# A two-layer diffusion-transformer step: modulation matmuls between the input's transposes, and head norms with an operand in PSUM

## The chip, the cores and the metric

The kernel runs on one core of one Trainium2 chip. The metric is the device time of one execution in microseconds (us). A core has five engines that run their own instruction queues and meet through semaphores: TensorE (PE: matmuls and transposes, into PSUM), VectorE (DVE), ScalarE (ACT: activation functions, casts), GpSimd (POOL) and SyncE (SP, which here issues the DMAs). A measurement of this kernel is the median of several runs.

## The reference

The reference is one step of a hybrid diffusion backbone: two layers, 1024 sample tokens and 128 prompt tokens of width 1024, all in float32. What bears on the change:

```python
def _rms(x, g):
    y = xf * lax.rsqrt(jnp.mean(xf * xf, axis=-1, keepdims=True) + EPS)
    return (y * g).astype(x.dtype)

def _modulation(cvec, w, b):
    m = (jax.nn.silu(cvec) @ w + b)[:, None, :]
    return jnp.split(m, 6, axis=-1)

def _layer(x, mod, lw, ctx):
    sh1, sc1, g1, sh2, sc2, g2 = mod
    h = _rms(x, n1) * (1 + sc1) + sh1
    u_conv, qa, ka, va, qn, kn, vn = jnp.split(h @ w_in, idx, axis=-1)
    a_out = _conv_module(u_conv, dw_w, dw_b, ln_g, ln_b)
    qa = _rms(qa.reshape(B, L, GQA_HEADS, HEAD_DIM), aqg)
    ka = _rms(ka.reshape(B, L, GQA_KV_HEADS, HEAD_DIM), akg)
    qn = _rms(qn.reshape(B, L, NA_HEADS, HEAD_DIM), nqg)
    kn = _rms(kn.reshape(B, L, NA_HEADS, HEAD_DIM), nkg)
    ...
    x = x + g1 * (jnp.concatenate([a_out, b_out, c_out], axis=-1) @ w_out)
    h = _rms(x, n2) * (1 + sc2) + sh2
    x = x + g2 * (jnp.square(jax.nn.relu(h @ w1)) @ w2)
```

So the modulation (a vector-matrix product with a 1024 x 6144 weight, for the sample's and the prompt's conditioning) must be known before the first projection, and every head of q and k is normalised by the root mean square of its 64 channels. The depthwise convolution has 31 taps over 256 channels.

## The kernel before

**Layout.** The residual X lies transposed in SBUF: 8 tiles (one for each 128 channels, index k) with all 1152 tokens along the free dimension. Tokens form three segments: si 0 and si 1 with 512 sample tokens each, si 2 with the 128 prompt tokens. Matmuls run on operands split in a high part and a low part (`wh`, `wl`, `HA` tiles): ACT casts the high part, and another engine subtracts it to get the low part (`split`, L155 on). The tiles come from pools with a fixed number of slots (S, T, U, V in SBUF; eight PSUM banks under one tag, `P`). A new tile waits until the slot's last user is done.

**The order** of instructions on each engine is the order of the Python program: there is no scheduler. Generators are advanced by `next` where their piece of work is to stand, and every engine works through its own queue in that order.

**The prologue** (`prologue`, L343) does the following, in this order.

- It issues the loads: four tiles `xt` with the first half of the sample, four `xh` with the second half (in slots HF 8 to 11 of a set of 16 buffers), two `xtp` for the prompt, then the weight of the first third of the modulation (`ada_w`, 16 loads of 512 KB into the HF buffers). As `xh` and the last four of these 16 share buffers, the last loads wait until PE has transposed `xh`.
- `x_in` (L331) brings in a segment. For each of 8 k: PE transposes 4 blocks (1 for the prompt) into a PSUM tile `psx`, VectorE copies it to X (L338), and `Norm.add` squares X on ACT and adds the square to an accumulator. There are two accumulators `nacc` a segment, for even and odd k. The even one is added by POOL, the odd one by VectorE; the first square of each is written to it directly.
- `modulation(0, [0], True)` (L183) multiplies: 8 steps of 4 matmuls into `psmod` (2 rows each). Then VectorE copies `psmod` to `mt` (L229), PE transposes it to `psmt`, VectorE adds the bias (`mod`) and forms `A1`.
- `Norm.rstd` (L272) adds the two accumulators, sums over the channels with a matmul against ones (`psn`), takes Ln and Exp on ACT (`rsq_start`), and improves the root in three VectorE operations (`rsq_end`).
- `pr.prep` splits weight tiles for the first projection (`wr` to `wh`, `wl`); the first is split with POOL. Then `norm1` writes the normalised input (`nx`, `HA`), and the first projection (`psf`) starts.

The order is: all of `x_in` for the three segments, then four modulation steps, the norms' matmuls, four more modulation steps; meanwhile ACT and VectorE take the roots.

**The projection** (`project`, L689) of a layer has 35 groups: seven column blocks (`ORDER`: A0 to A5, VN) x five token groups (`GROUPS`: four of 256 tokens, one of 128). A group is a chain of matmuls into `pst` (L541 to L543). For 30 of the groups `post` calls `head_stats` and `head_norm` (L415, L425): ACT squares `pst`, VectorE sums over each head (`ss`, L420), ACT takes Ln and Exp into `y`, VectorE improves the root in three small operations on 128x8 or 128x4 elements (`nt`, `y`) and multiplies (`xn`, L99). POOL applies gains and the rotary tables (`o`), and the result goes to DRAM (`ddA`), from where the attention reads it back (`kd`).

Between the two halves of `post` stand the taps of the convolution (`conv_tap`): on VectorE a scalar_tensor_tensor over 128x1167 (`cacc`), and for 22 taps of the second channel half an ACT product (`cp`) with an addition on POOL (L570). Every second group advances `fill`, the modulation of the remaining two thirds, by one step (`aw` loads, `psmod`, `mt`, `psmt`).

`rsq_end`, which the head norms and the token norms share, is:

```python
    def rsq_end(q, y, t, m):
        stt(t, y, -0.5 / m, y, ALU.mult, ALU.mult)
        stt(t, q, EPS * m, t, ALU.add, ALU.mult)
        stt(y, t, 1.5, y, ALU.add, ALU.mult)
```

Of the kernel before, what the change touches and what calls it, by code (L numbers as in the profile page):

```python
# [14 lines left out]
ACTF = mybir.ActivationFunctionType  # L15
ALU = mybir.AluOpType
# [9 lines left out]
DH = 64  # L26
EPS = 1e-6
# [18 lines left out]
def hybrid_step(ctx, tc, I, O, depth=DEPTH):  # L46
    nc = tc.nc
# [10 lines left out]
    def S(shape, dt=F32, n="s"):  # L58
        return pers.tile([128] + list(shape), dt, tag="S", bufs=N_S, name=nm(n))
# [7 lines left out]
    def V(shape, n="v"):  # L67
        return pers.tile([128] + list(shape), F32, tag="V", bufs=24, name=nm(n))
# [18 lines left out]
    def P(n="ps"):  # L87
        return psum.tile([128, 512], F32, tag="p", bufs=8, name=nm(n))
# [3 lines left out]
    def act(out, in_, func, scale=1.0, bias=0.0, **k):  # L92
        nc.scalar.activation(out=out, in_=in_, func=func, scale=scale, bias=bias, **k)  # L93
# [7 lines left out]
    def stt(out, a, s, b, op0, op1):  # L101
        nc.vector.scalar_tensor_tensor(out=out, in0=a, scalar=s, in1=b, op0=op0, op1=op1)  # L102
# [7 lines left out]
    eps = pers.tile([128, 1], F32, name="eps")  # L110
# [32 lines left out]
    def load(out, in_, eng=None):  # L143
        (eng or nc.sync).dma_start(out=out, in_=in_)
# [17 lines left out]
    def rsq_start(q, y, m):  # L162

        act(y, q, ACTF.Ln, scale=1.0 / m, bias=eps)
        act(y, y, ACTF.Exp, scale=-0.5)
# [6 lines that stand above are left out]
# [11 lines left out]
    def modulation(l, groups, first=False):  # L183

        todo = [(r, k) for r in groups for k in range(KT)]
        ready = []

        def fetch():
            if todo:
                r, k = todo.pop(0)  # L190
                if first:
                    if k % 2 == 0:
                        o = {0: 0, 2: 12, 4: 4, 6: 8}[k]
                        ready.extend([[HF[o + 2 * a + b][:, c:c + 512] for b in range(2) for c in (0, 512)] for a in range(2)])
                    o = {0: 0, 2: 12, 4: 4, 6: 8}[k - k % 2] + 2 * (k % 2)
                    for b in range(2):
                        c = r * 2048 + b * 1024
                        load(HF[o + b][:, 0:1024], I["ada_w"][l, k * 128:(k + 1) * 128, c:c + 1024])
                    return
                four = []  # L200
                for c in range(r * 2048, (r + 1) * 2048, 512):
                    aw = T([512], n="aw")
                    load(aw, I["ada_w"][l, k * 128:(k + 1) * 128, c:c + 512])
                    four.append(aw)
                ready.append(four)

        for _ in range(6 if first else 1):
            fetch()
        if first:
            ps = P("psmod")  # L210
            nc.vector.memset(ps, 0.0)
            yield
            fetch()
            fetch()
        yield
        for r in groups:
            if not first:
                ps = P("psmod")
                nc.vector.memset(ps, 0.0)
                yield  # L220
            for k in range(KT):
                aw = ready.pop(0)
                for j in range(4):
                    mm(ps[32 * j:32 * j + 2, :], silc[:, k, :], aw[j], start=(k == 0), stop=(k == KT - 1))
                if not first:
                    fetch()
                yield
            mt = T([512], n="mt")
            nc.vector.tensor_copy(mt, ps)  # L229
            yield  # L230
            pt = P("psmt")
            for b in range(4):
                nc.tensor.transpose(pt[:, b * 128:(b + 1) * 128], mt[:, b * 128:(b + 1) * 128], ident)
            ptv = pt.rearrange("p (b j x) -> p j b x", b=4, j=4, x=32)
            for s in range(2):
                tt(mod[l][:, s, r * 16:(r + 1) * 16].rearrange("p (j b) -> p j b", j=4), ptv[:, :, :, s],
                   ada_b(l)[:, r * 16:(r + 1) * 16].rearrange("p (j b) -> p j b", j=4), ALU.add)
            if r == 0:
                for s in range(2):
                    stt(A1[l][:, s, :], mod[l][:, s, 8:16], 1.0, n1g(l), ALU.add, ALU.mult)  # L240
            if r == 2:
                for s in range(2):
                    stt(A2[l][:, s, :], mod[l][:, s, 32:40], 1.0, n2g(l), ALU.add, ALU.mult)
            yield
# [75 lines left out]
    def run(g):  # L320
        for _ in g:
            pass
# [8 lines left out]
    def x_in(si, xt, nrm):  # L331

        n = SEGS[si][1]
        for k in range(KT):
            ps = P("psx")
            for i in range(n // 128):
                nc.tensor.transpose(ps[:, i * 128:(i + 1) * 128], xt(i, k), ident)
            nc.vector.tensor_copy(xs(k, si), like(si, ps[:, 0:n]))  # L338
            nrm.add(k)
            if k % 2:  # L340
                yield

    def prologue(pr):  # L343
        nc.scalar.preload_act_table_set("natural_log_exp_and_others")
        make_identity(nc, ident)
        nc.vector.memset(ones, 1.0)
        nc.vector.memset(eps, EPS)
        cc = U([KT, 2], n="cc")
        xt = [S([1024], n="xt") for _ in range(4)]
        for i in range(4):  # L350
            load(xt[i], I["x_sample"][i * 128:(i + 1) * 128, :])
        load(cc, I["cc"])
        load(vecs[0], I["vecs"][0])
        xh = [HF[8 + i][:, 0:1024] for i in range(4)]
        for i in range(4):
            load(xh[i], I["x_sample"][(i + 4) * 128:(i + 5) * 128, :])
        xp = [T([512], n="xtp") for _ in range(2)]
        for b in range(2):
            load(xp[b], I["x_prompt"][:, b * 512:(b + 1) * 512])
        m0 = modulation(0, [0], True)  # L360
        next(m0)
        sg = U([KT, 2], n="sg")
        sigmoid_of(sg, cc)
        tt(silc, cc, sg, ALU.mult)
        norms = [Norm(si) for si in range(3)]
        for k in range(KT):
            X[k] = S([2, HT], n="X")
        run(x_in(0, lambda i, k: xt[i][:, k * 128:(k + 1) * 128], norms[0]))
        del xt
        run(x_in(1, lambda i, k: xh[i][:, k * 128:(k + 1) * 128], norms[1]))  # L370
        next(m0)
        pr.fetch()
        pr.fetch()
        run(x_in(2, lambda i, k: xp[k // 4][:, k % 4 * 128:(k % 4 + 1) * 128], norms[2]))
        del xp
        for _ in range(4):
            next(m0)
        gs = [nrm.rstd() for nrm in norms]
        for _ in range(2):
            for g in gs:  # L380
                next(g)
        run(gs[0])
        for _ in range(2):
            next(m0)
        pr.prep(nc.gpsimd)
        for _ in range(2):
            pr.fetch()
        load(colmask, I["colmask"])
        for l in range(1, depth):
            load(vecs[l], I["vecs"][l])  # L390
        spill(0, 0)
        spill(0, 1)
        run(m0)
        first = norm1(pr.L, 0, norms[0], True)
        next(first)
        pr.prep()
        run(first)
        for g in gs[1:]:
            run(g)
        pr.prep()  # L400
        yield
        yield from together(norm1(pr.L, 2, norms[2], True), norm1(pr.L, 1, norms[1], True))
# [12 lines left out]
    def head_stats(x, nt):  # L415
        n = nt * (x.shape[2] // 64)
        sq = T([nt, x.shape[2]], n="sq")
        act(sq, x, ACTF.Square)
        ss = V([n], "ss")
        nc.vector.tensor_reduce(out=ss, in_=sq.rearrange("p t (h d) -> p (t h) d", d=64), op=ALU.add, axis=AX.X)  # L420
        y = V([n], "y")
        rsq_start(ss, y, DH)
        return x, nt, n, ss, y

    def head_norm(x, nt, n, ss, y):  # L425
        rsq_end(ss, y, V([n], "nt"), DH)
        w = x.shape[2]
        xn = T([nt, w], n="xn")
        tt(heads4(xn, nt), heads4(x, nt), y.rearrange("p (t h) -> p t h", t=nt).unsqueeze(3).to_broadcast([128, nt, w // 64, 64]), ALU.mult)
        return xn  # L430
# [1365 lines left out]
    def spill(l, t):  # L1796
        for k in range(KT):
            load(dx[l][:, k, t * HT:(t + 1) * HT], X[k][:, t, :])
# [12 lines left out]
    with tc.manual_schedule():  # L1811
        L = begin_layer(0)
        pr = Projection(L)
# [3 lines left out]
        for l in range(depth):  # L1817
# [22 lines left out]
            pr = Projection(N)  # L1840
# [142 lines left out]
```

## Time and profile before

| | us |
|---|---|
| median of 3 runs | 2981.17 |
| lowest, highest | 2978.42, 2985.02 |
| the profiled execution | 2982.7 |
| its span, first to last instruction | 2980.9 |
| prologue's last accumulator addition ends | 36.2 |
| first ACT write of the normalised input (`HA`) | 47.17 |
| first matmul of the first projection (`psf`) | 47.94 |
| projection's token groups, layer 0 | about 105 to 360 |
| projection's token groups, layer 1 | about 1600 to 1850 |

PE's mean granted clock over the span is 0.983 of full speed. The page's times are those of one execution; a span of the trace is 1.8 us shorter than what the execution was timed at.

In the rows of the profile, `mt<-psmod` reads: writes mt, reads psmod; then come partitions x elements and the type, and how many such instructions were merged in the row. A bracket at a row's end gives the idle time of the engine ahead of it and what ended it. In a group's row, three durations are the shortest, the median and the longest in ns.

### The profile page before, as it was taken

How to read it: one execution, taken by the hardware profiler on the slowest of the kernel's cores; microseconds unless marked ns; L12 is line 12 of the kernel's file. 1: busy time of each engine (PE TensorE's matmuls, PEld its weight loads, DVE VectorE, ACT ScalarE, POOL GpSimd, SP SyncE). 2: the span in 40 equal slices, each digit the busy share in tenths (PEclk: the TensorE clock that was granted, in tenths of full speed). 3: DMA queues.
4: the chain of work that ended last, by engine and by line, in shares of the span. 5: the costliest groups of instructions: out<-in, count | busy, mean ns of one | idle time of the engine just before them, and what ended most of it. 6: DMA issues, size and time to landing. Idle time of an engine off the chain costs nothing.

```text
span 2980.9 us, 52857 instructions
## 1 busy us (share of the span) xinstructions
PE 2844.0 (95%) x20328; PEld 2525.2 (85%) x20328; DVE 2096.1 (70%) x4009; ACT 1401.0 (47%) x2864; POOL 652.5 (22%) x607
## 2 busy tenths in 40 slices
PE   6998999999999999999889989999999999999999
PEld 3878745789999989999868886458999999999999
DVE  6588778764867756768675877788557677585676
ACT  4333356762744443433452353668537444433343
POOL 3576345420000000000224772463100000000000
PEclk8999999999999999999999999999999999999999
DMA  7276302424466678443333672024245666565334
GB/s 286 85 210 167 106 20 61 102 65 139 148 212 198 208 239 300 161 156 96 122 129 106 187 200 75 16 55 111 89 124 179 207 203 196 201 236 183 116 102 161
DMA packets 434876, 444.05 MB, mean 149 GB/s; under 512 B 120512, under 2 KB 308672, under 8 KB 434624
## 3 DMA queue, kind: packets, MB, share of 16 engines
q1 hardware_dynamic: 434624, 440.67, 47.4%
q8 instruction: 160, 2.62, 0.4%
q14 instruction: 92, 0.75, 0.1%
HBM read 307.41 MB, written 133.17 MB: 148 GB/s over the span
## 4 chain that ended last, share of the span: by engine, by line
PE 76%; DVE 13%; ACT 4%; issue 2%; DMA 2%; POOL 2%; SPq 1%; DVEq 0%; POOLq 0%; ACTq 0%
PE ps L1319 23%; PE psb L1319 8%; PE psc L1319 6%; PE pso L1319 5%; PE psa L1319 5%; PE psd L1319 3%; PE psacc L1118 3%; PE pspv L985 2%; DVE cacc L102 2%; PE pspt L969 2%; PE pst L541 2%; PE pst L542 2%; PE pst L543 2%; PE psst L1132 2%; PE psm L1044 2%
## 5 line engine op out<-in xcount | busy, mean ns | idle before, releaser
L1319 PE MATMUL ps<-ts,w2h 128*128 128x288 f32 x3072 | 534.4, 296 | 8.3 <-DVE ts L99 4.8
L1319 PEld LDWEIGHTS ps<-ts,w2h 128*128 128x128 f32 x3072 | 451.7, 189 | 9.3 <-DVE ts L99 5.3
L1319 PE MATMUL ps<-ts,w2l 128*128 128x288 f32 x1536 | 329.2, 295 | 0.1
L96 ACT CAST ts<-ti 128x576 fp32r<-128x576 f32 x256 | 172.1, 672 | 310.2 <-PE ps L1319 208.6
L541 PE MATMUL pst<-wh,HA 128*128 128x256 f32 x1040 | 297.9, 286 | 0.0
L542 PE MATMUL pst<-wl,HA 128*128 128x256 f32 x1040 | 294.3, 283 | 0.2 <-DVE wl L99 0.2
L543 PE MATMUL pst<-wh,HA 128*128 128x256 f32 x1040 | 293.7, 282 | 0.0
L93 ACT ACTIVATE ev<-ev 128x576 f32<-128x576 f32 x240 | 164.7, 686 | 265.1 <-DVE ev L99 261.3
L1319 PEld LDWEIGHTS ps<-ts,w2l 128*128 128x128 f32 x1536 | 247.6, 189 | 0.4 <-DVE w2l L99 0.3
L102 DVE SCALAR_TENSOR_TENSOR X<-ps,mod,X 128x288 f32<-128x288 f32 x336 | 112.2, 410 | 163.5 <-PE ps L1319 163.5
L99 DVE TENSOR_TENSOR ts<-ti,ts 128x576 fp32r<-128x576 f32 x256 | 195.5, 764 | 44.7 <-ACT ts L96 44.7
L541 PEld LDWEIGHTS pst<-wh,HA 128*128 128x128 f32 x1040 | 198.3, 191 | 19.2 <-issue 6.9
L542 PEld LDWEIGHTS pst<-wl,HA 128*128 128x128 f32 x1040 | 198.2, 191 | 0.5 <-DVE wl L99 0.4
L543 PEld LDWEIGHTS pst<-wh,HA 128*128 128x128 f32 x1040 | 198.2, 191 | 0.0
L99 POOL TENSOR_TENSOR nacc<-nacc,nsq 128x512 f32<-128x512 f32 (+1 forms) x12 | 15.8, 1320 | 822.2 <-PE ps L1319 796.3
L1772 POOL COPY yu<-X 128x128 f32<-128x128 f32 x8 | 3.9, 500 | 836.2 <-DVE X L102 824.3
L1319 PE MATMUL pso<-HA,woh 128*128 128x288 f32 x1024 | 177.8, 295 | 0.0
L1046 DVE TENSOR_REDUCE mx<-psm 128x1 f32<-128x384 f32 x288 | 142.3, 547 | 30.1 <-PE psm L1044 30.0
L93 ACT ACTIVATE pt<-psst 128x512 f32<-128x512 f32 x216 | 118.1, 597 | 89.6 <-PE psst L1133 88.7
L99 POOL TENSOR_TENSOR R<-R,pt 128x1024 f32<-128x1024 f32 x60 | 148.3, 2472 | 26.3 <-ACT pt L93 24.3
L1319 PEld LDWEIGHTS pso<-HA,woh 128*128 128x128 f32 x1024 | 149.7, 188 | 0.0
L102 DVE SCALAR_TENSOR_TENSOR cacc<-cin,vecs,cacc 128x1167 f32<-128x1167 f32 x78 | 136.8, 1754 | 11.3 <-POOL cacc L570 10.1
(279 smaller groups left out, 7222.6 us busy)
## 6 DMA issues: line engine op xcount, KB each, us to landing
ti<-hd SPq DMA_DIRECT2D x128, 576.0 KB, 4.0
hd<-ev SPq DMA_DIRECT2D x224, 288.0 KB, 4.2
w1r<-in_mlp_w SPq DMA_DIRECT2D x176, 256.0 KB, 4.0
aw<-in_ada_w SPq DMA_DIRECT2D x160, 256.0 KB, 4.0
HF<-in_mlp_w SPq DMA_DIRECT2D x128, 256.0 KB, 5.3
ddA<-o SPq DMA_DIRECT2D x144, 128.0 KB, 3.0
wr<-in_w_in SPq DMA_DIRECT2D x28, 512.0 KB, 4.1
sd<-ev SPq DMA_DIRECT2D x24, 576.0 KB, 2.8
```

The costliest lines, as they stand in the source:

```text
L93: nc.scalar.activation(out=out, in_=in_, func=func, scale=scale, bias=bias, **k)
L96: nc.scalar.copy(out, in_)
L99: (eng or nc.vector).tensor_tensor(out=out, in0=a, in1=b, op=op)
L102: nc.vector.scalar_tensor_tensor(out=out, in0=a, scalar=s, in1=b, op0=op0, op1=op1)
L541: mm(o, hi, wh, start=(k == 0), stop=False)
L542: mm(o, hi, wl, start=False, stop=False)
L543: mm(o, lo, wh, start=False, stop=(k == KT - 1))
L969: nc.tensor.transpose(ps[0:n, c], self.p[j][:, o:o + n], ident)
L985: mm(ps[64 * j:64 * j + 64, 0:128], v[j], self.at[j, i], start=(i == 0), stop=(i == nb - 1))
L1046: nc.vector.tensor_reduce(out=mx[j][:, qt, b:b + 1], in_=ps[:, 0:384], op=ALU.max, axis=AX.X)
L1118: mm(acc[64 * j:64 * j + 64, :], v, pt[:, j, :], start=(kt == 0), stop=(kt == 8))
L1319: mm(ps[h][:, 0:HH], x, y[:, h * HH:(h + 1) * HH], start=(start and z == 0), stop=(stop and z == 2), skip_group_check=True)
```

## The change

In the prologue, `xh` gets four tiles of its own, so that all modulation loads can be issued at once. The modulation's steps stand between pairs of k of the second and third `x_in`: four steps in the second segment, two in the third, and two later. The norms' additions both go to VectorE. The accumulators of the first segment are added before the third `x_in`; the other two follow after it, then all Ln and Exp. The first weight split goes from POOL to VectorE and ahead of the first segment's three root operations.

In the head norms a PSUM tile `pss` holds two small pieces, `z` and `t`. ACT writes the root a second time, to `z`; each of VectorE's three operations then has one input in SBUF and one in PSUM.

```diff
@@ modulation
-        for _ in range(6 if first else 1):
+        for _ in range(7 if first else 1):
             fetch()
         if first:
             ps = P("psmod")
             nc.vector.memset(ps, 0.0)
             yield
-            fetch()
             fetch()
@@ prologue
-        xh = [HF[8 + i][:, 0:1024] for i in range(4)]
+        xh = [S([1024], n="xh") for _ in range(4)]
@@
-        norms = [Norm(si) for si in range(3)]
+        norms = [Norm(si, (nc.vector, nc.vector)) for si in range(3)]
         for k in range(KT):
             X[k] = S([2, HT], n="X")
         run(x_in(0, lambda i, k: xt[i][:, k * 128:(k + 1) * 128], norms[0]))
         del xt
-        run(x_in(1, lambda i, k: xh[i][:, k * 128:(k + 1) * 128], norms[1]))
+        pr.fetch()
         next(m0)
         pr.fetch()
-        pr.fetch()
-        run(x_in(2, lambda i, k: xp[k // 4][:, k % 4 * 128:(k % 4 + 1) * 128], norms[2]))
+        for _ in x_in(1, lambda i, k: xh[i][:, k * 128:(k + 1) * 128], norms[1]):
+            next(m0)
+        del xh
+        gs = [nrm.rstd() for nrm in norms]
+        next(gs[0])
+        for i, _ in enumerate(x_in(2, lambda i, k: xp[k // 4][:, k % 4 * 128:(k % 4 + 1) * 128], norms[2])):
+            if i % 2:
+                next(m0)
         del xp
-        for _ in range(4):
-            next(m0)
-        gs = [nrm.rstd() for nrm in norms]
-        for _ in range(2):
-            for g in gs:
-                next(g)
-        run(gs[0])
-        for _ in range(2):
-            next(m0)
-        pr.prep(nc.gpsimd)
         for _ in range(2):
             pr.fetch()
         load(colmask, I["colmask"])
         for l in range(1, depth):
             load(vecs[l], I["vecs"][l])
+        next(gs[1])
+        next(gs[2])
+        for g in gs:
+            next(g)
+        next(m0)
+        pr.prep()
+        run(gs[0])
+        next(m0)
         spill(0, 0)
@@ head_stats, head_norm
         y = V([n], "y")
-        rsq_start(ss, y, DH)
-        return x, nt, n, ss, y
-
-    def head_norm(x, nt, n, ss, y):
-        rsq_end(ss, y, V([n], "nt"), DH)
+        small = P("pss")
+        z, t = small[:, 0:n], small[:, 64:64 + n]
+        act(y, ss, ACTF.Ln, scale=1.0 / DH, bias=eps)
+        act(z, y, ACTF.Exp, scale=-0.5)
+        act(y, y, ACTF.Exp, scale=-0.5)
+        return x, nt, n, ss, y, z, t
+
+    def head_norm(x, nt, n, ss, y, z, t):
+
+        stt(t, y, -0.5 / DH, z, ALU.mult, ALU.mult)
+        stt(z, ss, EPS * DH, t, ALU.add, ALU.mult)
+        stt(y, z, 1.5, y, ALU.add, ALU.mult)
```

VectorE's queue in the first `x_in`, from the fourth block on, before (X are the residual's tiles, `psx` the transposed blocks, `nsq` ACT's squares, the number behind a name tells tiles of one name apart):

```order
L338 COPY X_176<-psx_206 128x512
L99 TENSOR_TENSOR nacc_195<-nacc_195,nsq_212 128x512
L338 COPY X_177<-psx_215 128x512
L338 COPY X_178<-psx_224 128x512
L99 TENSOR_TENSOR nacc_195<-nacc_195,nsq_230 128x512
L338 COPY X_179<-psx_233 128x512
L338 COPY X_180<-psx_242 128x512
L99 TENSOR_TENSOR nacc_195<-nacc_195,nsq_248 128x512
```

The same place on VectorE with the change, from the third block on:

```order
L337 COPY X_181<-psx_203 128x512
L99 TENSOR_TENSOR nacc_193<-nacc_193,nsq_209 128x512
L337 COPY X_182<-psx_212 128x512
L99 TENSOR_TENSOR nacc_201<-nacc_201,nsq_218 128x512
L337 COPY X_183<-psx_221 128x512
L99 TENSOR_TENSOR nacc_193<-nacc_193,nsq_227 128x512
L337 COPY X_184<-psx_230 128x512
L99 TENSOR_TENSOR nacc_201<-nacc_201,nsq_236 128x512
```

Before, two copies stand between additions, and the even accumulator is not in this queue; now each copy is followed by an addition of the square that was made from it.

VectorE's queue behind the prompt's blocks, up to the copy of `psmod`, before (the accumulators' sums, then the first segment's root, then the copy `mt`):

```order
L99 TENSOR_TENSOR nacc_187<-nacc_187,nacc_195 128x512
L99 TENSOR_TENSOR nacc_257<-nacc_257,nacc_265 128x512
L99 TENSOR_TENSOR nacc_334<-nacc_334,nacc_339 128x128
L102 SCALAR_TENSOR_TENSOR nt_411<-rstd_398 128x512
L102 SCALAR_TENSOR_TENSOR nt_411<-psn_396,nt_411 128x512
L102 SCALAR_TENSOR_TENSOR rstd_398<-nt_411,rstd_398 128x512
L229 COPY mt_459<-psmod_165 128x512
```

The same with the change:

```order
L99 TENSOR_TENSOR nacc_271<-nacc_271,nacc_279 128x512
L99 TENSOR_TENSOR nacc_355<-nacc_355,nacc_360 128x128
L99 TENSOR_TENSOR wl_436<-wr_257,wh_435 128x1024
L102 SCALAR_TENSOR_TENSOR nt_439<-rstd_418 128x512
L102 SCALAR_TENSOR_TENSOR nt_439<-psn_416,nt_439 128x512
L102 SCALAR_TENSOR_TENSOR rstd_418<-nt_439,rstd_418 128x512
L228 COPY mt_463<-psmod_171 128x512
```

The first segment's sum has moved ahead of the prompt's blocks, and the split `wl` of the first weight tile, which needs ACT's cast `wh`, now stands ahead of the root.

In layer 0's projection, a piece of VectorE's queue that ends at the copy `mt` of the modulation's second third, before:

```order
L420 TENSOR_REDUCE ss_2344<-sq_2342 128x8
L102 SCALAR_TENSOR_TENSOR cacc_1084<-cin_668,vecs_100,cacc_1084 128x1167 x2
L102 SCALAR_TENSOR_TENSOR nt_2354<-y_2346 128x8
L102 SCALAR_TENSOR_TENSOR nt_2354<-ss_2344,nt_2354 128x8
L102 SCALAR_TENSOR_TENSOR y_2346<-nt_2354,y_2346 128x8
L99 TENSOR_TENSOR xn_2358<-pst_2292,y_2346 128x512
L229 COPY mt_2361<-psmod_1171 128x512
```

And with the change:

```order
L423 TENSOR_REDUCE ss_2365<-sq_2363 128x8
L102 SCALAR_TENSOR_TENSOR cacc_1091<-cin_672,vecs_100,cacc_1091 128x1167 x2
L102 SCALAR_TENSOR_TENSOR pss_2368<-y_2367,pss_2368 128x8
L102 SCALAR_TENSOR_TENSOR pss_2368<-ss_2365,pss_2368 128x8
L102 SCALAR_TENSOR_TENSOR y_2367<-pss_2368,y_2367 128x8
L99 TENSOR_TENSOR xn_2380<-pst_2313,y_2367 128x512
L228 COPY mt_2383<-psmod_1178 128x512
```

The order is the same; each of the three small operations now reads one operand from the PSUM tile. On ACT, one activation more (`pss<-y`) stands between the Ln and the Exp of each head norm.

## The prediction

> **What bounds the kernel now.** I read the page's busy shares first, then PE's waits by releaser, then the stages, then the two places where PE stands still. The first row says that TensorE sets the time: it is busy for 2844.0 of 2980.9 us. So an edit counts only where it moves PE's start, closes a hole in PE's row, or opens one.
>
> ```profile
> PE 2844.0 (95%) x20328; PEld 2525.2 (85%) x20328; DVE 2096.1 (70%) x4009; ACT 1401.0 (47%) x2864; POOL 652.5 (22%) x607
> ```
>
> The change touches the prologue (to about 50 us) and the 60 head norms, which stand in each layer's projection: 105 to 360 us in layer 0, 1600 to 1850 in layer 1. These are PE's waits there, layer 0 in the first fence and layer 1 in the second (total, times, longest):
>
> ```profile
> PE psmod L224 <- DMA aw<-in_ada_w: 5.9, 5, 1.7
> PE psmt L233 <- DVE mt L229: 5.7, 1, 5.7
> PE pstr L784 <- DMA kd<-ddA: 3.1, 1, 3.1
> ```
> ```profile
> PE psmt L233 <- DVE mt L229: 5.9, 2, 5.5
> PE psmod L224 <- DMA aw<-in_ada_w: 4.8, 4, 1.7
> PE pstr L784 <- DMA kd<-ddA: 2.4, 1, 2.4
> ```
>
> The largest hole is the same in both: PE must transpose `mt`, a copy that stands on VectorE behind the head norms, and VectorE is late. In the DVE rows ahead of it (start, duration) a 128x8 operation takes 2.71 us, although the row above does the same size in 0.15; the POOL row, last, explains it: a conv addition started 10 ns earlier and ended 20 ns before it.
>
> ```profile
> 230.59 0.15 DVE L102 SCALAR_TENSOR_TENSOR nt<-y 128x8 f32<-128x8 f32 x1
> 230.78 2.71 DVE L102 SCALAR_TENSOR_TENSOR nt<-ss,nt 128x8 f32<-128x8 f32 x1
> ...
> 242.04 0.68 DVE L229 COPY mt<-psmod 128x512 f32<-128x512 f32 x1
> ```
> ```profile
> 230.77 2.70 POOL L570 TENSOR_TENSOR cacc<-cacc,cp 128x1167 f32<-128x1167 f32 x1 [1.32 <-ACT cp L93]
> ```
>
> The groups by form (ns: shortest/median/longest) say which operations can be held up so. Both inputs in SBUF: up to 2679, against 147. One input in PSUM: the 60 `xn`, between the same POOL operations, never over 693, and the 14 `nt<-psn,nt` never over 692. That is the row on which the head-norm edit rests.
>
> ```profile
> L102 DVE SCALAR_TENSOR_TENSOR nt<-y x60: 147/223/2679, 120.4 to 1785.5; 128x8 f32<-128x8 f32 x32, 128x4 f32<-128x4 f32 x24, 128x2 f32<-128x2 f32 x4
> L99 DVE TENSOR_TENSOR xn<-pst,y x60: 291/691/693, 121.0 to 1790.2; 128x512 f32<-128x512 f32 x32, 128x256 f32<-128x256 f32 x24, 128x128 f32<-128x128 f32 x4
> L102 DVE SCALAR_TENSOR_TENSOR nt<-rstd x14: 217/680/693, 40.1 to 2247.7; 128x512 f32<-128x512 f32 x8, 128x64 f32<-128x64 f32 x4, 128x128 f32<-128x128 f32 x2
> L102 DVE SCALAR_TENSOR_TENSOR nt<-psn,nt x14: 224/691/692, 40.9 to 2248.0; 128x512 f32<-128x512 f32 x8, 128x64 f32<-128x64 f32 x4, 128x128 f32<-128x128 f32 x2
> L93 ACT ACTIVATE y<-y x60: 203/208/211, 117.5 to 1785.2; 128x8 f32<-128x8 f32 x32, 128x4 f32<-128x4 f32 x24, 128x2 f32<-128x2 f32 x4
> L570 POOL TENSOR_TENSOR cacc<-cacc,cp x42: 2647/2707/3835, 190.3 to 1793.4; 128x1167 f32<-128x1167 f32 x42
> L102 DVE SCALAR_TENSOR_TENSOR cacc<-cin,vecs,cacc x78: 1417/1436/3715, 133.4 to 1833.9; 128x1167 f32<-128x1167 f32 x78
> ```
>
> By stages, for tile `nt` alone (DVE busy, then count), and then for all engines (PE, PEld, DVE, ACT, POOL, each with its count; then granted clock):
>
> ```profile
> 105.00:360.00 255.00, 47.96 (x90) 0.97 0.58 160
> ```
> ```profile
> 194.00:243.00 49.00, 43.28 (x363) 40.12 (x362) 46.55 (x50) 18.73 (x36) 28.84 (x14) 0.97 0.63 173
> 240.00:250.00 10.00, 7.13 (x45) 7.16 (x46) 9.68 (x15) 3.61 (x7) 4.30 (x3) 0.66 0.25 55
> 250.00:288.00 38.00, 35.77 (x298) 32.58 (x296) 30.99 (x42) 16.05 (x29) 29.27 (x14) 1.00 0.74 191
> 288.00:295.00 7.00, 6.15 (x30) 6.18 (x31) 3.46 (x6) 4.19 (x7) 5.08 (x3) 0.51 1.03 287
> 1718.00:1728.00 10.00, 5.83 (x39) 5.86 (x40) 9.68 (x15) 2.49 (x7) 3.87 (x3) 0.83 0.30 65
> ```
>
> So the three small operations of layer 0's 30 head norms hold VectorE for 47.96 us. At 0.17 each they would need about 15, so 33 us are waiting for POOL. And a hole in PE is followed by a slow clock: 45 matmuls at the 0.120 us of the stage from 250 (35.77/298) would be 5.4 us, not 7.13, so 1.7 go after `psmt`; in the same way 6.15 - 3.6 = 2.5 after `kd`, and 5.83 - 4.7 = 1.1 in layer 1.
>
> **Part 1, head norms.** Ninety operations a layer leave the competition with POOL. VectorE does not win 33 us by that, since its next two-input operation, a tap (`cacc`) or a split (`wl`), meets the same POOL addition. I bound it from both sides. From 194 to 243 the two engines were taking turns nearly all the time: POOL's 28.84; eleven VectorE taps at 1.42, 15.6; three splits at about 1.2, 3.6; seven head norms at 3 x 0.17, 3.6; together 51.6 of 49 us, POOL's figure containing a few us of its own waits. Lower bound: turns stay full, and only the 3.6 us come back. Upper bound: POOL's additions fall behind (nobody waits for them until the conv ends) and `mt` is in time: the whole 5.7. I take **4.8** in layer 0 and **4.5** of 5.5 (same lower bound) in layer 1, nearer the top because `xn` and the reduction, 1.3 us a group, now run beside POOL's addition too. With the hole short, most of its slow clock goes: **1.5** of 1.7 and **1.0** of 1.1, lower end 0.
>
> The `kd` load waits for POOL's outputs, which follow `xn`. If PE comes 6.3 earlier, POOL must too, and by 3.1 more to close the hole. In its stage POOL is busy 29.27 of 38 us, so it has room, while VectorE's waiting in front of `xn` goes. I take **2.0** of 3.1 and **1.5** of the 2.5 for the clock, and **1.6** of 2.4 in layer 1; lower end 0. The `aw` holes (10.7 in both layers) hang on loads whose buffers come free from the same tiles: **1.0**, between 0 and 2. Sum 17.9; lower ends 7.2; upper ends 24.
>
> Costs: 60 more activations on ACT at 0.208 (row `y<-y`), 12.5 us on an engine that is busy 18.73 of 49 us there. Where VectorE waits for ACT it is 0.2 later; only the last one before a hole counts, so **0.5** in all; with every one on the path it would be 12.5. No row has such an operation that also writes PSUM; reading it costs 7 ns at 64 elements (224 against 217), so I take nothing, and bound it by 60 x 3 x 0.01, 2 us. The PSUM tile makes each head norm hold one of eight banks until its `y` is done, so PE's `pst` waits for a `y` of two to four groups earlier; with before's times the margins are positive but for one of 0.3 us, so I take 0, with 2 as the upper end.
>
> [...]
>
> **Part 2, prologue.** The change puts psmod's 64 matmuls between transposes and both halves of the norm's additions on VectorE. The rows: VectorE, then ACT, then PE.
>
> ```profile
> 16.62 1.33 DVE L99 TENSOR_TENSOR nacc<-nacc,nsq 128x512 f32<-128x512 f32 x1 [0.70 <-ACT nsq L93]
> 17.88 1.28 DVE L338 COPY X<-psx 128x512 f32<-128x512 f32 x2
> 19.86 1.32 DVE L99 TENSOR_TENSOR nacc<-nacc,nsq 128x512 f32<-128x512 f32 x1 [0.70 <-ACT nsq L93]
> ...
> 34.37 0.52 DVE L99 TENSOR_TENSOR nacc<-nacc,nsq 128x128 f32<-128x128 f32 x1 [0.38 <-ACT nsq L93]
> ...
> 35.66 0.52 DVE L99 TENSOR_TENSOR nacc<-nacc,nsq 128x128 f32<-128x128 f32 x1 [0.38 <-ACT nsq L93]
> 36.10 1.48 DVE L99 TENSOR_TENSOR nacc<-nacc,nacc 128x512 f32<-128x512 f32 x3
> ...
> 43.38 0.69 DVE L229 COPY mt<-psmod 128x512 f32<-128x512 f32 x1 [1.09 <-PE psmod L224]
> ```
> ```profile
> 18.59 1.23 ACT L93 ACTIVATE nsq<-X 128x512 f32<-128x512 f32 x2 [2.00 <-DVE X L338]
> ...
> 38.76 0.69 ACT L93 ACTIVATE rstd<-psn,eps 128x512 f32<-128x512 f32 x1 [3.13 <-PE psn L277]
> ...
> 40.02 0.67 ACT L93 ACTIVATE rstd<-psn,eps 128x512 f32<-128x512 f32 x1
> ...
> 41.85 1.03 ACT L96 CAST wh<-wr 128x1024 fp32r<-128x1024 f32 x1
> 47.17 0.72 ACT L93 ACTIVATE HA<-nx,mod 128x512 fp32r<-128x512 f32 x1 [4.29 <-DVE nx L102]
> ```
> ```profile
> 32.63 4.97 PE L224 MATMUL psmod<-HF,silc 128*2 128x512 f32 x32
> ```
>
> Before, two blocks take 3.24 us (16.62 to 19.86): two copies run through, two squares follow, VectorE adds one while POOL adds the other. In the new order VectorE has copy, addition, copy, addition, and each addition waits for the square of the copy just ahead: the next copy is queued behind that wait, and PE's transposes behind it for want of a bank. A block is then 0.71 (copy to square) + 0.63 + 0.03 + 0.60 (one of the three undisturbed additions) = 1.97 us, not 1.62. Six blocks of each half pay: 2 x 6 x 0.35 = 4.2; the moved `nacc` addition 0.6; the prompt's three pairs (1.29 each, 34.37 to 35.66) by the same ratio, 1.22, 0.9: the last addition ends at about 42.0 instead of 36.18, **+5.8**. Two additions remain, to 43.0. Before, ACT's first Ln came 1.2 after the additions; now its second does, at about 44.3 (45.2 if PE has the half clock). From there to the cast `wh` took 1.83 (40.02 to 41.85), so the cast starts at 46.1. Behind it VectorE now has the split (1.2; it was on POOL, off the path) and the three root operations (2.1), so `mt` starts at 46.1 + 1.03 + 1.2 + 2.1 = 50.4, 7.0 late. The first `nx` ran at 1.7 beside POOL's and will run alone, which returns 1.0. Psmod itself, 4.97 and 3.6 us of PE, leaves the path, but it stood beside ACT's roots. Sum **+6.0**, with the half clock +6.9; I take **+6.5**, bounds +3 (an addition hidden somewhere) and +8. From 87 us PE runs on without holes, so the shift is carried to the end. Two pairs of `wr` loads now wait for the last transpose of `xh`, at about 36; the queue ahead of them lands at about 40, so nothing behind them is late.
>
> **Sum.** The profiled run took 2982.7 us, 1.8 around its span and 1.5 above the median of the three runs, 2981.17. 2982.7 - 17.9 + 0.5 + 6.5 = 2971.8; against the median about 2971.
>
> **Rivals.** (a) *The turns stay full.* Taps and splits take over the waits; each layer gets the 3.6 and no clock: -7.2 + 0.5 + 6.5, time 2981. For it: 51.6 of 49 us; against it: nothing makes POOL keep pace. (b) *Nothing comes back, slower.* POOL's next addition, no longer held up by three small operations, starts earlier, just ahead of a tap that stands before `mt`, and VectorE loses there what it won. It decides where `mt` starts no more than 1 us nearer to PE's arrival; that the small operations still wait although one operand is in PSUM ends the same way (against that, the 693 ns). Time 2981 + 7, 2988. (c) *Prologue free.* If the additions find gaps after all, or the shift is swallowed before 87 us, psmod's removal shows: +0 instead of +6.5 and the head norms near their upper end: 2960 to 2964. Against it: the order of VectorE's rows leaves no gap.
>
> **How the numbers follow.** Forecast 0.50, its own range 2966 to 2977; (a) 0.19; (b) 0.15; (c) 0.16. The range 2960 to 2988 leaves out the outer parts of (b) and (c). Same means within 0.2% of 2981.17 (2975.2 to 2987.1), about what a measurement of this kernel can tell. Faster: (c) and most of the forecast, 0.62. Same: (a) and the edge of the forecast, 0.23. Slower: (b), 0.15.
>
> **What would show it.** In the profile after: block period 1.97 and first `HA` activation at 53 to 54 for the prologue; longest `pss` and `y` operations of the head norms under 0.3 us; the `psmt` hole under 2 us in both layers, `cacc` and `wl` longer on average (the inherited waits); the clock from 240 to 250 near 1. The prediction is wrong if `psmt` keeps 4 us or more, if `pst` shows waits for a bank, or if the first `HA` is not late.

## The result, and the profile after

The changed kernel takes 2965.7 us (median of 4 runs, 2962.11 to 2966.74) against 2983.1 for the kernel before (4 runs): a ratio of 0.9941, 95% interval 0.9923 to 0.9958, that is 17 us or 0.6% less. The profiled execution took 2966.74, its span is 2965.0.

The first row of the page, as before, has PE's busy time first. It has hardly moved (2844.0 before), so what went is time in which PE stood still. VectorE's busy time has fallen by 59.5 us.

```profile
PE 2847.9 (96%) x20328; PEld 2523.7 (85%) x20328; DVE 2036.6 (69%) x4019; ACT 1414.1 (48%) x2924; POOL 647.5 (22%) x597
```

PE's waits in the projections, layer 0 (105 to 360 us) and then layer 1 (1590 to 1850), with total, times and longest:

```profile
PE psmod L223 <- DMA aw<-in_ada_w: 5.3, 6, 1.6
PE psmu L739 <- DVE cacc L102: 3.2, 1, 3.2
PE psnm L1045 <- DVE nmx L1039: 2.3, 1, 2.3
PE pstr L794 <- ACT sq L93: 0.4, 1, 0.4
```
```profile
PE psnm L1045 <- DVE nmx L1039: 4.8, 2, 2.5
PE psmod L223 <- DMA aw<-in_ada_w: 3.9, 4, 1.3
PE psmu L739 <- DVE cacc L102: 0.8, 1, 0.8
PE pstr L794 <- ACT sq L93: 0.5, 1, 0.5
PE psmt L232 <- DVE mt L228: 0.3, 1, 0.3
```

The `psmt` hole (5.7 and 5.5 us before) and the `kd` hole (3.1 and 2.4) are gone in both layers, but for 0.3 at `psmt` and 0.4 and 0.5 at `pstr`. The rows `psmu` and `psnm` are not new: before has the same waits there, with 3.2 at `psmu` just behind 360 us and 2.3 and 4.8 at `psnm`. The groups by form (ns: shortest, median, longest) show that none of VectorE's 180 small operations is held up any more. In the trace of before 29 of them last over 1 us, and each of these ends 15 to 26 ns after an operation of POOL ends: what they waited for was POOL.

```profile
L93 ACT ACTIVATE pss<-y x60: 175/180/182, 127.0 to 1769.4; 128x8 f32<-128x8 f32 x32, 128x4 f32<-128x4 f32 x24, 128x2 f32<-128x2 f32 x4
L102 DVE SCALAR_TENSOR_TENSOR pss<-y,pss x60: 150/163/172, 129.9 to 1769.9; 128x8 f32<-128x8 f32 x32, 128x4 f32<-128x4 f32 x24, 128x2 f32<-128x2 f32 x4
L102 DVE SCALAR_TENSOR_TENSOR pss<-ss,pss x60: 165/170/171, 130.1 to 1770.1; 128x8 f32<-128x8 f32 x32, 128x4 f32<-128x4 f32 x24, 128x2 f32<-128x2 f32 x4
L102 DVE SCALAR_TENSOR_TENSOR y<-pss,y x60: 159/166/166, 130.3 to 1770.3; 128x8 f32<-128x8 f32 x32, 128x4 f32<-128x4 f32 x24, 128x2 f32<-128x2 f32 x4
```

In layer 0 they now keep VectorE busy for 14.81 us instead of 47.96 (first fence, tile `pss`: VectorE, then ACT). The stages around the old holes, in the second fence with the columns of before (PE, PEld, DVE, ACT, POOL, each with its count; then the granted clock), show a PE without holes at full clock; the stage from 240 had 7.13 us of PE and a clock of 0.66:

```profile
105.00:360.00 255.00, 14.81 (x90) 5.36 (x30) 0.99 0.59 162
```
```profile
194.00:243.00 49.00, 48.77 (x389) 42.91 (x390) 35.78 (x54) 22.93 (x48) 35.67 (x22) 1.00 0.81 221
240.00:250.00 10.00, 10.00 (x88) 10.00 (x87) 9.60 (x15) 4.94 (x9) 7.09 (x3) 1.00 0.56 137
1718.00:1728.00 10.00, 10.00 (x88) 9.59 (x90) 7.97 (x15) 3.80 (x9) 9.37 (x4) 1.00 0.83 226
```

The prologue has become longer. These are its rows on VectorE and then on ACT:

```profile
18.68 0.69 DVE L99 TENSOR_TENSOR nacc<-nacc,nsq 128x512 f32<-128x512 f32 x1 [0.69 <-ACT nsq L93]
19.29 0.68 DVE L337 COPY X<-psx 128x512 f32<-128x512 f32 x1
20.67 0.69 DVE L99 TENSOR_TENSOR nacc<-nacc,nsq 128x512 f32<-128x512 f32 x1 [0.70 <-ACT nsq L93]
...
48.44 1.23 DVE L99 TENSOR_TENSOR wl<-wr,wh 128x1024 fp32r<-128x1024 f32 x1 [4.94 <-ACT wh L96]
...
51.64 0.68 DVE L228 COPY mt<-psmod 128x512 f32<-128x512 f32 x1
```
```profile
47.38 1.03 ACT L96 CAST wh<-wr 128x1024 fp32r<-128x1024 f32 x1
54.27 0.72 ACT L93 ACTIVATE HA<-nx,mod 128x512 fp32r<-128x512 f32 x1 [5.87 <-DVE nx L102]
```

An addition is 1.99 us behind the last one (18.68 to 20.67), an idle 0.70 of it waiting for the square; the first `HA` activation comes at 54.27 instead of 47.17, 7.10 late. Followed along PE's row, matched by its instructions, the shift against before runs so: first matmul of the first projection 7.1 (55.04 for 47.94); first token group 9.4; behind layer 0's projection, at 342 us of before, -3.9; at the second layer's projection -4.6; behind it -16.1; at the end -16.0. So the prologue costs 7.1, layer 0's projection returns 13.3, layer 1's 11.5. The 2.3 between the first projection and the token groups come under a granted clock of 0.82 where before had 0.88; of them 1.1 at most return in the runs below.

### The profile page after: what moved, and what is told of

It reads as the page before. It is cut to its first block, busy times and chain, and to the rows that moved or that the text cites. A ratio compares the mean times of both kernels' runs of the same rounds, so it can differ in the third digit from the quotient of the medians.

```text
span 2965.0 us, 52903 instructions
## 1 busy us (share of the span) xinstructions
PE 2847.9 (96%) x20328; PEld 2523.7 (85%) x20328; DVE 2036.6 (69%) x4019; ACT 1414.1 (48%) x2924; POOL 647.5 (22%) x597
## 4 chain that ended last, share of the span: by engine, by line
PE 82%; DVE 9%; ACT 3%; POOL 2%; issue 2%; DMA 1%; SPq 0%; DVEq 0%; POOLq 0%; ACTq 0%
PE ps L1329 23%; PE psb L1329 8%; PE psc L1329 7%; PE pso L1329 5%; PE psa L1329 5%; PE pst L551 3%; PE pst L552 3%; PE pst L553 3%; PE psd L1329 3%; PE psacc L1128 3%; PE pspv L995 2%; PE pspt L979 2%; PE psst L1142 2%; PE psm L1054 1%; PE pstr L794 1%
## 5 line engine op out<-in xcount | busy, mean ns | idle before, releaser
L99 POOL TENSOR_TENSOR nacc<-nacc,nsq 128x512 f32<-128x512 f32 x3 | 6.9, 2299 | 793.8 <-PE ps L1329 793.7
```

Source lines behind the costliest of these rows:

```text
L99: (eng or nc.vector).tensor_tensor(out=out, in0=a, in1=b, op=op)
```

## The experiments

All comparisons are with the kernel before, on one chip for each group of runs. The first four take the two parts of the change, and the parts of the head norm, one by one.

**Head norms alone** (the head-norm part of the diff above on the kernel before).

> Before's prologue with the head norms of the change. Theory (waits of two-input operations for POOL go when one input is in PSUM): the whole gain is here, 22 to 27 us below before, ratio 0.991 to 0.993; longest pss and y operation under 0.2 us; no psmt hole over 1 us and no kd hole over 1 us in either layer; first HA activation at 47.2 as before. Rival (the gain needs the later start of the projections, that is another phase between POOL and VectorE): 10 us or less below before, psmt hole 2 us or more.

Measured: 2961.64 against 2983.98, ratio 0.9924 (0.9899 to 0.9949). In its trace the same two waits read 0.3 for `psmt` in either layer; `kd` is gone in layer 0 and 1.4 in layer 1, somewhat over what was expected. This part alone returns 22 us by the medians, 5 more than the whole change, and the rival that wanted the later start falls. The first `HA` activation comes at 47.92: four traces with the prologue of before have it between 46.81 and 48.02, so its time is good to about 1 us.

**Prologue alone** (the prologue's part of the diff, the head norms of before).

> The prologue of the change with the head norms of before. Theory (each addition waits for its own square, and the split stands ahead of the roots): first HA activation at 54.3, 7.1 late, and with the longer slow clock behind it some 9 us at the first token group; the end is 7 to 10 us later than before, ratio 1.0023 to 1.0035. Rival (the shift is swallowed by the psmt holes of the projection, since VectorE and POOL start later together with PE): within 3 us of before.

Measured: 2987.85 against 2983.98, ratio 1.0015 (1.0002 to 1.0028): slower, by less than expected, though the interval takes in the lower end. It reaches below the rival's 3 us as well (0.6 to 8 us), so the time alone does not decide between the two; the trace does. In the trace the first matmul of the first projection comes 6.9 late and the first token group 6.7, and the shift is still 6.5 at 343 us of before. So the `psmt` hole swallows nothing:

```profile
PE psmod L223 <- DMA aw<-in_ada_w: 6.1, 5, 1.9
PE psmt L232 <- DVE mt L228: 6.0, 2, 5.7
PE pstr L787 <- DMA kd<-ddA: 3.8, 1, 3.8
```

The extra 2.3 us of the changed kernel's trace ahead of the token groups are absent here, with the same prologue: the stage takes 59.1 us, as before, under a clock of 0.91. So the prologue does not bring them by itself. Later the shift of this trace wanders between 7 and -2, mostly in stages that no edit touches, and ends at -1.0; this execution is the fastest of the ten. The two parts add up: 0.9924 x 1.0015 = 0.9939, and the whole change had 0.9941.

**The second root, all in SBUF.**

```diff
-        small = P("pss")
-        z, t = small[:, 0:n], small[:, 64:64 + n]
+        z, t = V([n], "z"), V([n], "t")
```

(against the head norms of the change, on before's prologue)

> Before with the second root of the change, but with z and t in SBUF tiles: the same instructions in the same order, all of VectorE's operands in SBUF. Theory: the place of the operand decides, so nothing is gained: within 4 us of before, small operations up to 2.7 us long, psmt hole 4 to 7 us in both layers, stretched time in the three small operations over 25 us a layer. Rival (what helps is that the operations no longer read the tile they have just written, or no longer read one tile twice): as heads_only, 20 us or more below before.

Measured: 2981.33 against 2983.98, ratio 0.9992 (0.998 to 1.0003). The groups by form, from this run:

```profile
L102 DVE SCALAR_TENSOR_TENSOR t<-y,z x60: 147/280/2676, 119.9 to 1782.8; 128x8 f32<-128x8 f32 x32, 128x4 f32<-128x4 f32 x24, 128x2 f32<-128x2 f32 x4
L102 DVE SCALAR_TENSOR_TENSOR z<-ss,t x60: 161/167/1222, 120.1 to 1783.8; 128x8 f32<-128x8 f32 x32, 128x4 f32<-128x4 f32 x24, 128x2 f32<-128x2 f32 x4
L102 DVE SCALAR_TENSOR_TENSOR y<-z,y x60: 160/168/2637, 120.3 to 1784.5; 128x8 f32<-128x8 f32 x32, 128x4 f32<-128x4 f32 x24, 128x2 f32<-128x2 f32 x4
```

The instructions, their order and their dependencies are those of the change; only the tile's memory differs, and the long waits are back, with `psmt` holes of 4.0 and 3.9 us. With z and t in PSUM, on the same prologue, the ratio was 0.9924: where the operand lay decided. That the second activation is cheap is seen here as well: 60 of them cost nothing that can be measured (0.9992).

**No second root, only t in PSUM.**

```diff
         y = V([n], "y")
+        t = P("pss")[:, 0:n]
         rsq_start(ss, y, DH)
-        return x, nt, n, ss, y
+        return x, nt, n, ss, y, t
 
-    def head_norm(x, nt, n, ss, y):
-        rsq_end(ss, y, V([n], "nt"), DH)
+    def head_norm(x, nt, n, ss, y, t):
+        rsq_end(ss, y, t, DH)
```

> Before with only t in PSUM and no second root: the first small operation reads y twice from SBUF, the second and third have one input in PSUM. In the trace of before, the first of the three lost 15.8 us in layer 0 and 17.2 in layer 1 to stretching, the other two 18.1 and 16.7. Theory: the first still waits, up to 2.7 us at a time, the others never; between 8 and 18 us below before, psmt hole between 0 and 4 us. Rival (the extra activation is needless, as a wait in one operation spares it to the next): as heads_only or better. Other rival (one wait per head norm remains, whichever operation it falls on): within 4 us of before.

Measured: 2987.32 against 2983.98, ratio 1.0013 (1.0001 to 1.0026). My expectation of 8 to 18 us less was wrong; of the three, the rival with one remaining wait fits, with a result at its upper edge. The groups by form:

```profile
L102 DVE SCALAR_TENSOR_TENSOR pss<-y x60: 155/358/2685, 122.1 to 1789.7; 128x8 f32<-128x8 f32 x32, 128x4 f32<-128x4 f32 x24, 128x2 f32<-128x2 f32 x4
L102 DVE SCALAR_TENSOR_TENSOR pss<-ss,pss x60: 165/170/172, 122.3 to 1790.9; 128x8 f32<-128x8 f32 x32, 128x4 f32<-128x4 f32 x24, 128x2 f32<-128x2 f32 x4
L102 DVE SCALAR_TENSOR_TENSOR y<-pss,y x60: 159/166/167, 122.5 to 1791.1; 128x8 f32<-128x8 f32 x32, 128x4 f32<-128x4 f32 x24, 128x2 f32<-128x2 f32 x4
```

The first operation reads SBUF twice, writes PSUM, and waits up to 2685 ns; the other two never do. But a third of the 18.1 us that those two had lost in layer 0 came back at the first, whose stretched time (above its shortest duration) rose from 15.8 to 21.9 us; waits of over 1 us in the three together fell only from 14 to 11, 21 in both layers, and each of the 21 ends 26 to 38 ns after an operation of POOL. How it comes about is seen at one place of this run, on VectorE and then on POOL:

```profile
235.02 4.66 DVE L102 SCALAR_TENSOR_TENSOR cacc<-cin,vecs,cacc 128x1167 f32<-128x1167 f32 x2
239.60 2.64 DVE L102 SCALAR_TENSOR_TENSOR pss<-y 128x8 f32<-128x8 f32 x1
242.28 0.17 DVE L102 SCALAR_TENSOR_TENSOR pss<-ss,pss 128x8 f32<-128x8 f32 x1
```
```profile
238.41 3.80 POOL L571 TENSOR_TENSOR cacc<-cacc,cp 128x1167 f32<-128x1167 f32 x1
```

POOL's addition is there at 238.41, sits out the tap's end (3.80 instead of 2.65), and gets its turn between the tap and the small operation, which then waits for all of it. One two-input operation left behind the taps was enough to lose the turn. The layer's `psmt` hole fell to 3.5 and 3.7, but `kd` took 3.8 in layer 0 and the `aw` waits 6.3 and 6.9. Along PE's row, layer 0 gets about 2.5 us back at `psmt`, and loses about 2 ahead of it, among the `aw` loads, and 0.5 at `kd`. That this version came out a little slower rather than equal is not explained.

The last three keep the head norms of the change and take the prologue apart.

**The norms' additions shared with POOL again.**

```diff
-        norms = [Norm(si, (nc.vector, nc.vector)) for si in range(3)]
+        norms = [Norm(si) for si in range(3)]
```

> The changed kernel with the norms' additions again shared by POOL (even) and VectorE (odd). Theory (the additions' wait for their own squares costs 5.8 us, the split ahead of the roots most of the rest): a pair of blocks takes 3.2 us again, first HA activation between 47.5 and 50 instead of 54.27, and the end 4 to 7 us below the changed kernel, ratio to before 0.990 to 0.9935. Rival (the modulation's matmuls between the transposes are what is late): first HA activation within 1 us of 54.3.

Measured: 2960.44 against 2982.72, ratio 0.9918 (0.9895 to 0.9942); first `HA` activation at 48.14. Squares come in pairs 3.2 us apart again. One line returns 6.1 of the 7.1 us of the prologue, and the rival, which blamed the modulation's matmuls between the transposes, falls. The 1.0 that is left arises behind the cast `wh`, with the split still ahead of the roots: the cast starts at 40.79, earlier than before's 41.85, and the first `HA` activation follows 7.35 later, where before had 5.32. The interval overlaps that of the whole change (0.9923 to 0.9958), as does that of the next run, so the earlier start of the projection is shown, and that the end comes earlier than the changed kernel's is only made likely.

**The additions on VectorE, one block late.**

```diff
                 act(like(self.si, sq), x, ACTF.Square)
+                if self.engines[0] is nc.gpsimd:
+                    tt(self.acc[k % 2], self.acc[k % 2], sq, ALU.add, self.engines[k % 2])
+                else:
+                    self.flush_add()
+                    self.late = (k, sq)
+
+        def flush_add(self):
+            if self.late is not None:
+                k, sq = self.late
                 tt(self.acc[k % 2], self.acc[k % 2], sq, ALU.add, self.engines[k % 2])
+                self.late = None
 
         def rstd(self):
 
+            self.flush_add()
```

(for the prologue's norms; the others add at once, as before)

> The changed kernel, with VectorE's addition of a square put behind the next block's copy, so that ACT squares one block while VectorE copies the next. Theory (only the wait was dear, not the additions' place on VectorE): a block takes 1.2 to 1.3 us instead of 1.99, the accumulators are done at 31 to 36 instead of 43.5, the first HA activation comes at 44 to 47, and the end is 7 to 10 us below the changed kernel, ratio to before 0.988 to 0.992. Rival (loads set the pace there): the first HA activation stays above 50.

Measured: 2959.41 against 2982.72, ratio 0.9913 (0.9891 to 0.9935). ACT's rows in this run:

```profile
14.19 0.63 ACT L93 ACTIVATE nsq<-X 128x512 f32<-128x512 f32 x1 [0.76 <-DVE X L348]
15.39 0.63 ACT L93 ACTIVATE nsq<-X 128x512 f32<-128x512 f32 x1 [0.57 <-DVE X L348]
...
44.30 0.72 ACT L93 ACTIVATE HA<-nx,mod 128x512 fp32r<-128x512 f32 x1 [5.86 <-DVE nx L102]
```

In the first segment a block takes 1.20 us instead of 1.99 with the same additions on the same engine, and the first `HA` activation comes 10.0 earlier than in the changed kernel. So it was the wait that was dear, not the work. By the ratios the end is 8 us below the changed kernel, 6 by the medians, which come from two groups of runs; 7 to 10 were expected.

**The same, with the first segment's roots ahead of the weight split.**

```diff
-        pr.prep()
         run(gs[0])
+        pr.prep()
```

> As adds_late, and the first segment's three root operations ahead of the first weight split on VectorE. Theory: the split's wait for ACT's cast no longer stands ahead of the roots, so the first HA activation comes 1 to 3 us earlier than in adds_late, if the weight's load has not become the limit; then both are alike within 0.5 us. The end 0 to 3 us below adds_late.

Measured: 2953.04 against 2982.72, ratio 0.9901 (0.9877 to 0.9924): the best of all, 30 us below the kernel before. VectorE's and ACT's rows:

```profile
35.25 0.69 DVE L102 SCALAR_TENSOR_TENSOR nt<-rstd 128x512 f32<-128x512 f32 x1 [0.96 <-ACT rstd L93]
...
38.02 1.88 DVE L99 TENSOR_TENSOR wl<-wr,wh 128x1024 fp32r<-128x1024 f32 x1 [0.62 <-ACT wh L96]
```
```profile
42.46 0.72 ACT L93 ACTIVATE HA<-nx,mod 128x512 fp32r<-128x512 f32 x1 [4.47 <-DVE nx L102]
```

The first `HA` activation comes 1.84 earlier than in the run before it, as expected; 0.45 of that is there at the cast already (36.96 for 37.41), so the new order gives about 1.4. The end gained 6 us, where 0 to 3 were expected. The prologue accounts for 2 of them at most; along PE's row the traces lie 0.7 apart at the first token group and grow apart to 10 in stages that no edit touches. With intervals of some 7 us to either side the rest is not to be told from chance.

## Why the prediction was right, point by point

**The direction and the mechanism** were right. The time, 2965.7, lies 0.3 us below the forecast's own range, and nearer to that of rival (c) than to the 2971 of the sum; it is the late first `HA` activation that speaks for the forecast against (c). The row on which the head-norm part rested, that operations with one input in PSUM never ran long beside POOL, held for all 180 (172 ns at most), and the contrast between the run with z and t in SBUF (0.9992) and the one with them in PSUM (0.9924) shows that the operand's place is what counted.

**The size of the head norms** was the term that was off: 17.9 us less 0.5 in the sum, against 22.3 measured alone and 13.3 + 11.5 in the changed kernel's trace, at my upper end of 24. Along PE's row, the shift falls by 7.8 and 7.1 us in the two layers at `psmt` with the clock behind it (6.3 and 5.5 in the sum), and by 5.4 and 2.7 at `kd` (3.5 and 1.6). I had let the freed time be taken over by the next two-input operation, a tap or a split. It was taken over only to a small part. DVE's busy time in the taps (tile `cacc`, third pair of columns) and in the splits (tile `wl`, the same) in layer 0, before and after:

```profile
105.00:360.00 255.00, 1.12 (x2) 0.30 (x2) 70.35 (x40) 1.35 (x1) 59.93 (x21) 0.97 0.58 160
105.00:360.00 255.00, 149.10 (x524) 100.34 (x523) 20.64 (x12) 0.00 (x0) 0.97 0.58 160
```
```profile
105.00:360.00 255.00, 2.25 (x4) 0.59 (x4) 71.46 (x40) 1.35 (x1) 60.34 (x21) 0.99 0.59 162
105.00:360.00 255.00, 152.57 (x537) 101.11 (x537) 24.30 (x12) 0.00 (x0) 0.99 0.59 162
```

The taps have gained 1.1 us, the splits 3.7: 4.8 of the 33.2 us that the small operations gave up. The rest did not move, it vanished, and a place of the changed kernel's trace shows how, on VectorE and then on POOL:

```profile
235.98 0.17 DVE L102 SCALAR_TENSOR_TENSOR y<-pss,y 128x8 f32<-128x8 f32 x1
236.35 0.69 DVE L99 TENSOR_TENSOR xn<-pst,y 128x512 f32<-128x512 f32 x1 [0.20 <-DVE y L102]
238.64 0.69 DVE L423 TENSOR_REDUCE ss<-sq 128x8 f32<-128x512 f32 x1 [1.60 <-ACT sq L93]
239.24 3.38 DVE L102 SCALAR_TENSOR_TENSOR cacc<-cin,vecs,cacc 128x1167 f32<-128x1167 f32 x2
```
```profile
235.97 2.71 POOL L580 TENSOR_TENSOR cacc<-cacc,cp 128x1167 f32<-128x1167 f32 x1 [1.54 <-ACT cp L93]
```

POOL's addition runs from 235.97 to 238.68. VectorE finishes the head norm beside it, multiplies `xn`, and then has nothing to do until ACT has squared the next group: it is no longer behind PE. By the time the next tap comes here, POOL is done.

My lower bound, that turns which stay full return only the small operations' own 3.6 us, was wrong. The same piece of the program, from the `ss` at 194.62 (203.80 with the change) to the copy `mt`, holds eleven taps, two splits and thirteen operations of POOL; here it is before and after (PE, PEld, DVE, ACT, POOL):

```profile
194.62:242.04 47.42, 42.53 (x357) 39.33 (x355) 45.58 (x48) 18.35 (x35) 28.04 (x13) 0.98 0.64 176
```
```profile
203.80:243.80 40.00, 40.00 (x337) 37.02 (x336) 32.59 (x48) 19.64 (x42) 27.94 (x13) 1.00 0.77 209
```

It is 7.4 us shorter, and VectorE, which had 1.8 us of idle time in it, has 7.4. With every operation of VectorE that has both inputs in SBUF, and every one of POOL's, at its shortest duration, an estimate from the rows by form, the two engines claim about 45 of the 47.4 us before and about 40 of the 40.0 after. So the turns are no emptier than they were, and a sum of claims did not bound what comes back. The `kd` holes went but for 0.4 and 0.5, where I took two thirds.

**The prologue** was right, 7.1 against 6.5, by the steps of its sum: a block of 1.99 us for 1.97, the cast `wh` at 47.38 for 46.1 (47.0 with the half clock; the granted clock was 0.50 from 36 to 46 us), `mt` at 51.64 for 50.4 (51.3). One reading in it was not: that psmod stood beside the roots. In before's row the copy `mt` waited 1.09 us for psmod, behind the roots; the sum did not use it. That the shift is carried to the end is shown up to 343 us by the trace of the prologue alone, and as 4 us (0.6 to 8) by its times. Behind that it is open: PE does have holes after 87 us (before has 5.7 and 5.5 at `psmt`), and that trace ends without the shift.

**The rivals.** Of (a) the picture fits and the price does not: the turns stayed about full, and the time came back all the same. Nothing of (b) came; the prologue was not free (c), although the head norms came out as (c) wanted. The banks: PE's matmuls show no wait at `pst`. Two idle stretches of 0.9 us of the weight load are put down to `pss`, but layer 0 has eleven such stretches before and eleven after, so a wait for a bank is not shown. Reading PSUM cost next to nothing here, as the sum had it: the shortest durations of the three operations are 150, 165 and 159 ns with an input in PSUM, and were 147, 161 and 161 with all inputs in SBUF, a difference of 4 ns at most, within the 10 ns an operation of my bound.

## What to carry to other kernels

Look for short two-input operations that last much longer than their median: here, with up to 2707 ns for a median of 167, they showed where VectorE lost its turn to GpSimd. Moving one input of every operation in the chain to PSUM freed the chain (172 ns at most, ratio 0.9924), while moving it for two of three shifted part of the wait and gained nothing (up to 2685 ns at the first, ratio 1.0013). When one engine adds what another has squared, put the addition one block behind; in the same queue, right after its own copy, it made each block as long as the whole chain of engines (1.99 us against 1.20). And judge a prologue by the first instruction of the bound engine behind it: here 64 matmuls were moved off its end, and the first projection started 7.1 us later.

## What the runs showed of the hardware that I had not expected

- An output in PSUM did not help: an operation that reads SBUF twice and writes PSUM still waited for POOL, up to 2685 ns; with one input in PSUM and the same output it never took over 172.
- The turn passed. In the run with only t in PSUM, POOL's addition, which came up at 238.41 while VectorE ran two taps (235.02 to 239.68), got in between them and the next small operation, which took 2.64 us, although VectorE had no idle time there.
- ACT wrote its small tile to PSUM in 180 ns (median of 60), and the same operation to SBUF, in the run with z there, in 208.
